# Output norm of a hybrid mLSTM and attention layer: variance from a ScalarE square, sums from the residual additions, and a same-engine lag in the kernel's own planner

## Chip, cores and metric

The kernel runs on one core of one Trainium2 chip. The metric is the device time of one execution in microseconds; the median of 3 runs before the change is 1039.39 us (1038.61 to 1039.49). Engines are named as in the profile: PE is TensorE, DVE VectorE, ACT ScalarE, POOL GpSimd, SP SyncE, whose queue issues nearly all of the transfers.

## What is computed

One inference step of one decoder layer for a prompt of 1024 tokens and 8 decode samples, width 1024. The stream is normalised and projected (`w_in`); one half of the width goes through an mLSTM (4 heads, chunks of 128 tokens), the other through sparse attention with three branches (compressed, selected, window), merged by gates. Both halves, each times a SiLU gate, are joined to `mix` and go through the output projection. The end, which the change is mostly about, is

```python
def layer_norm(x, g=None, b=None):
    mu = xf.mean(-1, keepdims=True)
    var = jnp.square(xf - mu).mean(-1, keepdims=True)
    y = (xf - mu) * lax.rsqrt(var + LN_EPS)
    ...

def residual_out(x, mix, gate, w_out, b_out, ln_g, ln_b):
    y = mix @ w_out + b_out
    return layer_norm(DEEPNORM_ALPHA * x.astype(jnp.float32) + gate * y, ln_g, ln_b)
```

## The kernel before

The work is written as some hundred Python generators ("lanes"), each a piece of the layer: projections of a weight block, score and value pieces of the attention, chunks of the mLSTM, loads. A planner sets the order in which their instructions are written out, and so the order of every engine's queue. `Plan.note` (from line 247 on) keeps a planned clock for each engine. It advances an engine by the cost of the instruction, from the latest of the engine's own clock and the ends of the writers of its inputs, each with a lag (`LAG`, 0.08 to 0.2 us by the engine that wrote). `Lanes.run` takes, among the lanes in order of rank, the first that is ready at TensorE's planned clock, and runs it to its next `yield`; `yield [x]` means "go on when x is planned to be there". `sooner((V, ...), (G, ...))` gives an element-wise operation to VectorE or GpSimd, whichever is planned to be done with it first, so a different planned clock also moves work between the two. The helper at line 308 emits every instruction, so all rows of the profile carry that line, and instructions are told apart by their tiles.

TensorE's bulk is `mm<-hh,wh` and its two companions (`hl`, `wl`): fp32 products are made of three matmuls of high and low parts, so each weight block needs `wh` (a ScalarE copy) and `wl` (a subtraction on GpSimd or VectorE). In the first 900 us this projection is interleaved with attention (`sc`, `tp`, `oo`) and mLSTM chunks (`nd` is a chunk's output, normalised with an rsqrt in small steps, `rs_v`, `rs_y`, `rs_t`, on VectorE or GpSimd).

The merge of the samples' attention (`sample_merge`, from line 1439) has a matmul that spreads `vs`, a copy of the new key and value rows, over partitions. The copy is issued right before the matmul.

The output projection (`output`, from line 2336 on) runs at the end. The weights come in 8 slices of 128 rows: `wof` (load, then the product with the gate on VectorE or GpSimd), `woh` (ScalarE copy), `wol` (difference, VectorE or GpSimd). The prompt is 8 row tiles t of 128 tokens. For each tile and each half i of the contraction (i = 1 first) the `mix` tile is loaded, multiplied with the attention's or mLSTM's gate, and split into `mixh` (ScalarE) and `mixl` (VectorE or GpSimd). 24 matmuls of 512 columns make one half, 48 a tile. The order of tiles is i = 1 for tiles 0 to 2, i = 0 for them, then tiles 3 to 7 with both halves. `res_load` brings the residual `xr` and adds alpha and the bias (`xr<-xr,bo`). With i = 0 done, VectorE adds each 512-column piece of the PSUM sum to `xr`, and the lane `finish` does the norm: statistics of two pieces and an aggregate (`lnst`, `fmv`), an rsqrt in ten small operations (`rs_v` to `frs`), minus mean times rsqrt (`fnm`), ScalarE's Identity with scale and bias, the product with `lg` (VectorE or GpSimd), the addition of `lb` (GpSimd) and the store. Tile 7 takes its statistics piece by piece (`last_st`) and splits the last steps between engines. The samples (`smp`) go through the same `finish` with 8 rows.

Of the kernel before, what the change touches and what calls it, by code (L numbers as in the profile page):

```python
# [11 lines left out]
AF = mybir.ActivationFunctionType  # L12
ALU = mybir.AluOpType
# [130 lines left out]
class Plan:  # L144
# [2 lines left out]

    LAG = {"PE": 0.2, "ACT": 0.15, "DVE": 0.13, "POOL": 0.08, "DMA": 0.0}
    TO = {"PE": 0.07, "POOL": 0.03}
    TICK = 10.24 / 3  # L150

    def __init__(self):
# [94 lines left out]
    def note(self, kind, op, a, kw):  # L247
        aps = [x for x in a if isinstance(x, bass.AP)] + [x for k, x in kw.items() if isinstance(x, bass.AP)]
        out = kw.get("out", a[0] if a else None)
        outs = [out] + ([kw["accum_out"]] if "accum_out" in kw else [])  # L250
        if "in_offset" in kw and kw["in_offset"] is not None:
            aps.append(kw["in_offset"].ap)
        ins = list(aps)
        for o in outs:
            ins.pop(next(i for i, x in enumerate(ins) if x is o))
        eng = kind
        waits = [(self.clock[kind], kind, "")]
        for x in ins:
            for c in self.cells(x):
                for e in self.wrote.get(c, ()):  # L260
                    if not (kind == "PE" and e[1] == "PE"):
                        waits.append((self.after(e, kind), e[1], c))
        for x in aps:
            if x.space == PSUM or any(x is o for o in outs):
                for c in self.cells(x):
                    waits += [(self.after(e, kind), k, c) for k, es in self.used.get(c, {}).items() if k != kind
                              for e in es]
        load = kind == "DMA" or op == "indirect_dma_start"
        if load and len(self.begun[kind]) >= 8:
            waits.append((self.begun[kind][-8][0], "RING", ""))  # L270
        t = max(w[0] for w in waits)
        if load:
            size = out.free_size() * 4 * out.partition_size() / 360.0e3
            run = min(x.ap[-1][1] if x.ap[-1][0] == 1 else 1 for x in [out] + ins)
            if run < 128 and kind == "DMA":
                size *= 2
            self.clock[kind] = t + (1.04 if kind == "POOL" else 0.475)
            eng = "DMA"
            e = [0.0, eng]
            self.transfer(self.clock[kind] + 0.65, size, e)  # L280
            self.begun[kind].append(e)
        else:
            c = self.cost(kind, op, t, out, ins, len(outs) > 1)
            e = [t + c, kind]
            eng = kind
            self.clock[kind] = t + c
            self.step_end = max(self.step_end, self.after(e, "PE"))
        for x in outs:
            for c in self.cells(x):
                self.wrote[c] = (self.wrote.get(c, []) if eng == "DMA" else [])[-7:] + [e]  # L290
        for x in aps:
            for c in self.cells(x):
                u = self.used.setdefault(c, {})
                u[eng] = (u.get(eng, []) if eng == "DMA" else [])[-7:] + [e]
# [60 lines left out]
def build(ctx, tc, I, O, dbg=None):  # L355
# [38 lines left out]
    def bank(tag, hold=False):  # L394

        def first():
            return min(idle(b) for b in range(8))
        if first() > plan.clock["PE"]:
            yield first
        while first() >= BIG:  # L400
            yield first
        return take(tag, hold)
# [69 lines left out]
        return t  # L472


    def rsqrt_steps(dst, var, n, eps, rows=slice(0, 128), eng=None):

        E = eng or V
        v = W([128, 4], "rs_v", "rs_v", 4)[rows, :n]
        y = W([128, 4], "rs_y", "rs_y", 4, I32)[rows, :n]
        t = W([128, 4], "rs_t", "rs_t", 4)[rows, :n]  # L480
        E.tensor_scalar(v, var, eps, None, op0=ALU.add)
        yield
        E.tensor_scalar(y, v.bitcast(I32), -0.5, 1597463007.0, op0=ALU.mult, op1=ALU.add)
        E.tensor_scalar(v, v, -0.5, None, op0=ALU.mult)
        yf = y.bitcast(F32)
        for i in range(3):
            yield
            if E is V and n == 1:
                V.scalar_tensor_tensor(t, yf, v, yf, op0=ALU.mult, op1=ALU.mult)
            else:  # L490
                E.tensor_tensor(t, yf, yf, op=ALU.mult)
                yield
                E.tensor_tensor(t, t, v, op=ALU.mult)
            yield
            d = dst if i == 2 else yf
            if E is V:
                V.scalar_tensor_tensor(d, t, 1.5, yf, op0=ALU.add, op1=ALU.mult)
            else:
                E.tensor_scalar(t, t, 1.5, None, op0=ALU.add)
                E.tensor_tensor(d, t, yf, op=ALU.mult)  # L500
# [938 lines left out]
    def sample_merge():  # L1439
# [7 lines left out]
                             start=(w == 0), stop=(w == 1), skip_group_check=True)  # L1447
        sn = C([128, 2], "sn")
        V.tensor_scalar(sn, ps[:, 0:2], BN0, NS, op0=ALU.add, op1=ALU.mult)
        ps = yield from bank("sc")  # L1450
        vs = H([8, 2, 2, 64], "vs")
        V.tensor_copy(vs, skv[:, 1:3, :, 1, :])
        T.matmul(ps[:, 0:256], kc("rb8", 8), vs.rearrange("p a k d -> p (a k d)"), start=True, stop=True)
        T.matmul(ps[:, 256:280], kc("rb8", 8), GS[:, 8:32], start=True, stop=True)
        vn = H([128, 2, 2, 64], "vn")
# [774 lines left out]
    og = {}  # L2230
    woh, wol = [None] * 8, [None] * 8

    def finish(r, rows, dst, last=None):

        mv = W([128, 2], "fmv", "fmv", 3)[rows]
        rs = W([128, 1], "frs", "frs", 3)[rows]
        nm = W([128, 1], "fnm", "fnm", 3)[rows]
        yield [r]
        if last is None:
            ln_stats(r, mv, rows)  # L2240
        else:
            V.bn_aggr(mv, last.rearrange("p a b -> p (a b)"))
        yield
        rsqrt(rs, mv[:, 1:2], 1, 1e-5, rows)
        V.scalar_tensor_tensor(nm, mv[:, 0:1], -1.0, rs, op0=ALU.mult, op1=ALU.mult)
        yield
        n = 1024 if last is None else 320
        a, b = slice(0, n), slice(n, 1024)
        S.activation(r[:, a], r[:, a], AF.Identity, bias=nm, scale=rs)
        (sooner((V, 1.2), (G, 3.5)) if last is None else G).tensor_tensor(r[:, a], r[:, a], og["lg"][rows, a], op=ALU.mult)  # L2250
        G.tensor_tensor(r[:, a], r[:, a], og["lb"][rows, a], op=ALU.add)
        if last is not None:
            V.scalar_tensor_tensor(r[:, b], r[:, b], mv[:, 0:1], og["lg"][rows, b], op0=ALU.subtract, op1=ALU.mult)
            V.scalar_tensor_tensor(r[:, b], r[:, b], rs, og["lb"][rows, b], op0=ALU.mult, op1=ALU.add)
            yield [r[:, b]]
            dma(dst[:, b], r[:, b])
        yield [r[:, a]]
        dma(dst[:, a], r[:, a])
# [77 lines left out]
    def output():  # L2336
# [65 lines left out]
        for t, i in [(t, i) for i in (1, 0) for t in range(3)] + [(t, i) for t in range(3, 8) for i in (1, 0)]:  # L2402
            if i == 0:
                yield from done("floads")
                load(t + 3)
            yield from done("w%d" % (2 + 5 * i), "mix%s%d" % ("ab"[i], t))
            hi, lo = mix.pop((t, i))
            for x, (m, tag) in enumerate(PIECES[t == 7]):
                m, n = slice(*m), m[1] - m[0]
                if i:  # L2410
                    po[t, x] = (yield from bank(tag or (["sc", "mm"][t % 2] if t != 2 else ["sc", "oo"][x]), True))[:, 0:n]
                ps = po[t, x]
                for k in range(4):
                    w = 4 * i + k
                    T.matmul(ps, hi[:, k], woh[w][:, m], start=(w == 4), stop=False)
                    T.matmul(ps, hi[:, k], wol[w][:, m], start=False, stop=False)
                    T.matmul(ps, lo[:, k], woh[w][:, m], start=False, stop=(w == 3))
                    if k % 2:
                        yield 0
                if i == 0:  # L2420
                    yield from done("res%d" % t)
                    xr = mix[t]
                    V.tensor_tensor(xr[:, m], ps, xr[:, m], op=ALU.add)
                    free(ps)
                    if t == 7:
                        ln_part(xr, last_st, m)
                    yield 0
            if i == 0:
                flags.add("out%d" % t)
                lanes.add(1, finish(xr, slice(0, 128), O["y_prompt"][0, 128 * t:128 * t + 128],  # L2430
                                     last_st if t == 7 else None))

    lanes.add(0, begin())
    lanes.run()
# [36 lines left out]
```

## Time and profile before

| | |
|---|---|
| median of 3 runs | 1039.39 us |
| profiled execution | 1039.46 us, span 1037.6 us |
| granted clock, mean | 0.967 of full |
| TensorE busy | 959.7 us (92%) |
| VectorE busy | 717.2 us (69%) |
| ScalarE busy | 530.2 us (51%) |
| GpSimd busy | 286.5 us (28%) |

Busy time is the union of an engine's instructions. The averages hide that the stages differ: from 1013 us on TensorE has nothing to do, and VectorE, at 69% overall, is busy in nearly all of the last 100 us. "Idle before, releaser" on a row is the time that the engine stood still ahead of that instruction, and the tile that it waited for. A number with x on a row of small instructions counts equal neighbours.

### The profile page before, as it was taken

What the parts mean: (1) busy time and instruction counts of PE and PEld (TensorE: products, weight loads), DVE (VectorE), ACT (ScalarE), POOL (GpSimd) and SP (SyncE); (2) the same over time, 40 slices, a digit from 0 to 9 for tenths busy, and PEclk for the clock granted to TensorE, in tenths of its full rate; (3) what the DMA queues carried; (4) which work ended last, traced back from release to release, by engine and by line L of the source; (5) the groups of instructions that cost most, each with busy time, mean ns of one, the idle gap of its engine ahead of it and who ended that gap; (6) DMA issues with size and microseconds to landing.
All of it is one profiled execution on the core that took longest, in us unless ns stands there. A gap on an engine that the chain in (4) does not pass through costs nothing.

```text
span 1037.6 us, 20058 instructions
## 1 busy us (share of the span) xinstructions
PE 959.7 (92%) x7338; PEld 864.9 (83%) x7338; DVE 717.2 (69%) x2266; ACT 530.2 (51%) x1329; POOL 286.5 (28%) x362
## 2 busy tenths in 40 slices
PE   4997899999999989999999999999999899989990
PEld 3786897989888889899999998899998889967780
DVE  4859864072323477789777788878784738999996
ACT  3557752143344656676667786666773321231111
POOL 6216423111453000110131001131012524253563
PEclk9988899999999989999999999999999989989996
DMA  8943419413698715311105111012102326479502
GB/s 329 408 189 117 148 70 361 151 50 118 221 326 286 216 55 165 111 57 37 47 11 157 29 47 38 25 36 74 47 33 85 113 65 191 142 264 362 168 22 81
DMA packets 85334, 141.42 MB, mean 136 GB/s; under 512 B 11657, under 2 KB 58286, under 8 KB 85108
## 3 DMA queue, kind: packets, MB, share of 16 engines
q1 hardware_dynamic: 76020, 106.59, 31.2%
q0 software_dynamic: 9216, 33.56, 9.0%
q8 instruction: 58, 0.95, 0.4%
q14 instruction: 40, 0.33, 0.1%
HBM read 117.73 MB, written 28.15 MB: 141 GB/s over the span
## 4 chain that ended last, share of the span: by engine, by line
PE 57%; DVE 11%; DMA 4%; issue 2%; POOL 2%; ACT 1%; POOLq 0%; SPq 0%; DVEq 0%; ACTq 0%
PE mm L308 27%; PE sc L308 13%; PE tp L308 9%; PE oo L308 7%; DVE xr L308 2%; DMA wof<-in_w_out 1%; DMA pgs<-in_cache_slc_kv,idx 1%; DVE smp L308 1%; DVE lnst L308 1%; DVE rs_t L308 1%; POOL wol L308 1%; DMA mg<-mgd 1%; DVE mixl L308 1%; DMA pgs<-in_cache_win_kv 1%; DVE rs_y L308 0%
## 5 line engine op out<-in xcount | busy, mean ns | idle before, releaser
L308 PE MATMUL mm<-hh,wh 128*128 128x344 f32 (+1 forms) x840 | 286.3, 341 | 0.0
L308 PE MATMUL mm<-hl,wh 128*128 128x344 f32 (+1 forms) x840 | 270.4, 322 | 0.0
L308 PE MATMUL mm<-hh,wl 128*128 128x344 f32 x816 | 262.6, 322 | 0.0
L308 POOL TENSOR_TENSOR wl<-wf,wh 128x1024 fp32r<-128x1024 f32 (+1 forms) x35 | 82.5, 2356 | 505.0 <-ACT wh L308 389.6
L308 PEld LDWEIGHTS mm<-hh,wh 128*128 128x128 f32 (+1 forms) x840 | 158.8, 189 | 12.1 <-issue 10.5
L308 PEld LDWEIGHTS mm<-hl,wh 128*128 128x128 f32 (+1 forms) x840 | 158.9, 189 | 0.7
L308 PEld LDWEIGHTS mm<-hh,wl 128*128 128x128 f32 x816 | 155.1, 190 | 0.0
L308 PE MATMUL oo<-pt,VT 128*64 128x128 f32 x1056 | 70.1, 276 | 0.0
L308 PE MATMUL sc<-kst,qs 128*128 128x448 f32 (+6 forms) x208 | 69.5, 343 | 0.3 <-DVE pt L308 0.3
L308 PE MATMUL sc<-kst,ql 128*128 128x448 f32 (+6 forms) x208 | 65.5, 325 | 0.0
L308 PEld LDWEIGHTS oo<-pt,VT 128*64 128x64 f32 x1056 | 58.1, 137 | 6.4 <-issue 5.2
L308 DVE COPY pt<-tp 128x512 f32<-128x512 f32 (+1 forms) x87 | 54.8, 645 | 9.9 <-PE tp L308 9.7
L308 ACT ACTIVATE pw<-pw,nbs 128x64 f32<-128x64 f32 (+2 forms) x112 | 54.6, 489 | 12.6 <-DVE tot L308 6.4
L308 ACT ACTIVATE pt<-tp 128x512 f32<-128x512 f32 (+1 forms) x73 | 39.8, 558 | 40.6 <-PE tp L308 40.4
L308 ACT ACTIVATE pa<-pa,nbs 128x384 f32<-128x384 f32 (+1 forms) x88 | 50.9, 580 | 14.6 <-DVE pa L308 12.4
L308 ACT ACTIVATE xh<-tp 128x512 fp32r<-128x512 f32 x64 | 38.0, 595 | 35.2 <-PE tp L308 34.9
L308 DVE TENSOR_TENSOR xl<-tp,xh 128x512 fp32r<-128x512 f32 x64 | 42.8, 679 | 14.3 <-ACT xh L308 14.0
L308 PE MATMUL tp<-KA,pgx 128*128 128x128 f32 x256 | 43.3, 293 | 2.8 <-ACT pgx L308 1.9
L308 ACT ACTIVATE ti<-sc,PKT 128x129 f32<-128x129 f32 x28 | 10.3, 369 | 67.3 <-DVE cx L308 67.3
L308 ACT ACTIVATE pp<-pp,nbs 128x64 f32<-128x64 f32 (+3 forms) x72 | 32.2, 449 | 22.7 <-DVE nbs L308 21.3
L308 PE MATMUL sc<-xl,w1h 128*128 128x256 f32 x128 | 38.3, 299 | 5.0 <-DVE xl L308 5.0
L308 PEld LDWEIGHTS sc<-kst,qs 128*128 128x128 f32 x208 | 39.8, 191 | 3.3 <-DVE pt L308 1.0
(506 smaller groups left out, 2285.0 us busy)
## 6 DMA issues: line engine op xcount, KB each, us to landing
wf<-in_w_blk SPq DMA_DIRECT2D x34, 512.0 KB
wada<-in_w_ada SPq DMA_DIRECT2D x24, 512.0 KB
wof<-in_w_out SPq DMA_DIRECT2D x16, 512.0 KB
xt<-in_x_prompt SPq DMA_DIRECT2D x8, 512.0 KB
pgs<-in_cache_win_kv SPq DMA_DIRECT2D x8, 512.0 KB
qf<-qtd SPq DMA_DIRECT2D x32, 128.0 KB
mix<-mxd SPq DMA_DIRECT2D x16, 256.0 KB
mix<-gtd SPq DMA_DIRECT2D x16, 256.0 KB
```

Of the source, the lines that this page charges most:

```text
L308: return f(*a, **kw)
```

## The change

Four things, of which the last reaches furthest:

1. For prompt tiles 0 to 6 the residual addition becomes a `tensor_tensor_reduce`, which adds the PSUM piece to `xr` and also sums the result into `osum` (two instructions: the operation and the read of its accumulator). The mean comes from the two sums (one small VectorE operation, negated), the variance from a ScalarE Square with the negated mean as bias and a row sum into `fmv` (its other output, `sq`, is not used). `rsqrt_steps` gets a factor, 1/1024, for it. Statistics and aggregate are gone for these tiles; tile 7 and the samples keep them.
2. `finish` now waits, in the plan, for ScalarE's Identity before the `lg` product is placed.
3. In `sample_merge` the copy to `vs` is issued first, and its lane yields before it takes a PSUM bank and issues the matmul.
4. The planner counts a lag (`OWN`, 0.08 to 0.1 us) between dependent instructions of the same engine on ScalarE, VectorE and GpSimd. Before, such a dependence had the engine's `LAG` as any other; transfers and TensorE had and have their own rule.

```diff
@@ class Plan
     LAG = {"PE": 0.2, "ACT": 0.15, "DVE": 0.13, "POOL": 0.08, "DMA": 0.0}
     TO = {"PE": 0.07, "POOL": 0.03}
+
+    OWN = {"ACT": 0.1, "DVE": 0.09, "POOL": 0.08}
@@ Plan.note
                 for e in self.wrote.get(c, ()):
-                    if not (kind == "PE" and e[1] == "PE"):
+                    if e[1] != kind:
                         waits.append((self.after(e, kind), e[1], c))
+                    elif kind in self.OWN:
+                        waits.append((e[0] + self.OWN[kind], kind, c))
@@ rsqrt_steps
-        E.tensor_scalar(v, var, eps, None, op0=ALU.add)
+        if scale is None:
+            E.tensor_scalar(v, var, eps, None, op0=ALU.add)
+        else:
+            E.tensor_scalar(v, var, scale, eps, op0=ALU.mult, op1=ALU.add)
@@ sample_merge
-        ps = yield from bank("sc")
         vs = H([8, 2, 2, 64], "vs")
         V.tensor_copy(vs, skv[:, 1:3, :, 1, :])
+        yield [vs]
+        ps = yield from bank("sc")
         T.matmul(ps[:, 0:256], kc("rb8", 8), vs.rearrange("p a k d -> p (a k d)"), start=True, stop=True)
@@ finish
-    def finish(r, rows, dst, last=None):
+    def finish(r, rows, dst, last=None, sums=None):
...
+        if sums is not None:
+
+            V.tensor_scalar(mv[:, 0:1], sums[:, 0:1], sums[:, 1:2], -1.0 / 1024, op0=ALU.add, op1=ALU.mult)
+            yield [mv]
+            sq = R([128, 1024], "sq")
+            S.activation(sq, r, AF.Square, bias=mv[:, 0:1], accum_out=mv[:, 1:2])
+            yield [mv]
+            rsqrt(rs, mv[:, 1:2], 1, 1e-5, rows, scale=1.0 / 1024)
+            V.scalar_tensor_tensor(nm, mv[:, 0:1], 1.0, rs, op0=ALU.mult, op1=ALU.mult)
...
         S.activation(r[:, a], r[:, a], AF.Identity, bias=nm, scale=rs)
+        if last is None:
+            yield [r[:, a]]
@@ output
-                    V.tensor_tensor(xr[:, m], ps, xr[:, m], op=ALU.add)
+                    if x == 0:
+                        sums = W([128, 2], "osum", "osum", 3)
+                    if t == 7:
+                        V.tensor_tensor(xr[:, m], ps, xr[:, m], op=ALU.add)
+                        ln_part(xr, last_st, m)
+                    else:
+                        V.tensor_tensor_reduce(out=xr[:, m], in0=ps, in1=xr[:, m], scale=1.0, scalar=0.0, op0=ALU.add,
+                                               op1=ALU.add, accum_out=sums[:, x:x + 1])
                     free(ps)
-                    if t == 7:
-                        ln_part(xr, last_st, m)
```

The instructions' order changes on every engine, mostly from about 360 us on. Three places follow. The line number before an operation is the helper's, 308 before and 312 after.

TensorE around the matmul of `vs` (`knew` scores the samples' new keys, `kst` the prompt's window; KS and GS are constants and gates). Before:

```order
L308 MATMUL mm<-hh,wl 128x344
L308 MATMUL sc<-knew,qbd 32x1 x16
L308 MATMUL sc<-vs,KS 128x256
L308 MATMUL sc<-GS,KS 128x24
L308 MATMUL sc<-kst,qs 128x320
L308 MATMUL sc<-kst,ql 128x320
```

and after the change, where the row of `knew` stands 25 rows above that of `vs`:

```order
L312 MATMUL mm<-hh,wl 128x344
L312 MATMUL sc<-kst,qs 128x256
L312 MATMUL sc<-kst,ql 128x256
L312 MATMUL sc<-kst,qs 128x320
L312 MATMUL sc<-kst,ql 128x320
L312 MATMUL sc<-vs,KS 128x256
L312 MATMUL sc<-GS,KS 128x24
```

24 rows of other work, projection and window scores, now stand between them.

VectorE in the mLSTM chunk near 820 us (`mva` is the chunk's variance on its way through GpSimd's rsqrt, `vx` the next chunk's values). Before:

```order
L308 TENSOR_TENSOR mva<-mva,den 128x4
L308 COPY vx<-tp 128x4x128
L308 TENSOR_TENSOR wof<-wof,gate 128x1024
L308 TENSOR_TENSOR wol<-wof,woh 128x1024 x2
L308 TENSOR_TENSOR mva<-mva,den 128x4
L308 TENSOR_SCALAR nd<-nd,mmv,mva 128x128 x4
```

and now:

```order
L312 TENSOR_TENSOR mva<-mva,den 128x4
L312 COPY vx<-tp 128x4x128
L312 TENSOR_TENSOR mva<-mva,den 128x4
L312 TENSOR_SCALAR nd<-nd,mmv,mva 128x128 x4
L312 TENSOR_SCALAR qm<-tp,g_106 128x512
```

The weight product `wof` and one `wol` have moved ahead, one `wol` to GpSimd.

VectorE at the additions of tile 5 in the output projection. Before:

```order
L308 TENSOR_TENSOR xr<-mm,xr 128x512
L308 TENSOR_TENSOR smp<-smp,lg 8x1024
L308 TENSOR_TENSOR xr<-xr,lg 128x1024
L308 BN_STATS lnst<-xr 128x6 x2
L308 BN_AGGR fmv<-lnst 128x2
```

and now:

```order
L312 ISA xr,osum<-mm,xr 128x512
L312 ISA osum 128x1
L312 TENSOR_TENSOR xr<-xr,lg 128x1024
L312 ISA xr,osum<-mm,xr 128x512
L312 ISA osum 128x1
L312 TENSOR_TENSOR mixl<-mix,mixh 128x512 x2
L312 TENSOR_SCALAR fmv<-osum 128x1
L312 TENSOR_SCALAR rs_v<-fmv 128x1
```

The two `mixl` are those of tile 7; before they were GpSimd's. The mean and the first step of the rsqrt, which needs ScalarE's sum of squares, follow each other without a row between them.

## Rows read from the trace of the kernel before

**Rows 1.** Busy time by stage, core 0; the columns are named in the first line.
```profile
core 0: us, PE busy (x) PEld busy (x) DVE busy (x) ACT busy (x) POOL busy (x), PEclk, DMA share, GB/s
400.00:600.00 200.00, 199.09 (x1682) 185.45 (x1682) 152.49 (x624) 142.23 (x417) 29.70 (x66) 1.00 0.24 72
...
900.00:940.00 40.00, 34.96 (x164) 29.46 (x163) 37.81 (x68) 11.60 (x16) 17.77 (x9) 0.91 0.83 274
940.00:1000.00 60.00, 60.00 (x275) 45.82 (x274) 56.78 (x101) 10.41 (x14) 30.50 (x14) 1.00 0.58 194
1000.00:1020.00 20.00, 13.58 (x83) 11.89 (x81) 18.02 (x47) 3.73 (x3) 9.71 (x5) 0.94 0.16 63
```

**Rows 2.** TensorE's waits: what for, us in total, times, longest.
```profile
PE tp L308 <- DVE nd L308: 5.9, 2, 4.2
...
PE sc L308 <- DVE vs L308: 3.0, 1, 3.0
PE sc L308 <- POOL wol L308: 2.9, 1, 2.9
```

**Rows 3.** Timeline of VectorE around 365 us, and busy time and clock behind it.
```profile
361.03 0.23 DVE L308 CUSTOM_DVE_ANT_0 pp<-sc,CBT 128x64 f32<-128x64 f32 x1 [3.22 <-POOL wl L308]
...
365.30 0.27 DVE L308 COPY vs<-skv 8x256 f32<-8x256 f32 x1
...
365.60:372.20 6.60, 6.57 (x23) 6.33 (x24) 4.09 (x24) 2.85 (x10) 0.00 (x0) 0.50 0.00 1
```

**Rows 4.** Timelines of VectorE and GpSimd around 820 us, and the stretch behind them.
```profile
820.92 2.44 DVE L308 TENSOR_TENSOR wol<-wof,woh 128x1024 fp32r<-128x1024 f32 x2
826.33 1.20 DVE L308 TENSOR_TENSOR mva<-mva,den 128x4 f32<-128x4 f32 x1 [2.98 <-POOL mva L308]
...
821.06 1.14 POOL L308 TENSOR_TENSOR rs_t<-rs_y 128x4 f32<-128x4 f32 x1
...
824.09 0.20 POOL L308 TENSOR_TENSOR rs_t<-rs_y 128x4 f32<-128x4 f32 x1
...
829.20:840.50 11.30, 11.30 (x63) 11.28 (x62) 2.69 (x6) 0.57 (x1) 2.37 (x1) 0.83 0.28 95
```

**Rows 5.** Timeline of GpSimd around 917 us, and the stretch behind TensorE's wait.
```profile
916.67 3.34 POOL L308 TENSOR_TENSOR wol<-wof,woh 128x1024 fp32r<-128x1024 f32 x1 [4.54 <-ACT woh L308]
...
920.07:925.70 5.63, 5.63 (x14) 4.50 (x15) 5.50 (x13) 1.06 (x1) 3.56 (x2) 0.54 0.87 261
```

**Rows 6.** Timelines of the output projection: VectorE, then GpSimd.
```profile
942.68 0.69 DVE L308 TENSOR_TENSOR xr<-sc,xr 128x512 f32<-128x512 f32 x1 [1.09 <-PE sc L308]
...
949.00 1.28 DVE L308 BATCH_NORM_STATS2 lnst<-xr 128x6 f32<-128x512 f32 x2
...
950.43 4.55 DVE L308 TENSOR_TENSOR mixl<-mix,mixh 128x512 fp32r<-128x512 f32 x2
...
1005.04 0.68 DVE L308 TENSOR_TENSOR xr<-mm,xr 128x512 f32<-128x512 f32 x1
...
1022.93 0.68 DVE L308 TENSOR_TENSOR xr<-sc,xr 128x512 f32<-128x512 f32 x1
...
951.71 2.71 POOL L308 TENSOR_TENSOR xr<-xr,lb 128x1024 f32<-128x1024 f32 x1
...
999.06 2.55 POOL L308 TENSOR_TENSOR mixl<-mix,mixh 128x512 fp32r<-128x512 f32 x2
...
1030.08 1.39 POOL L308 TENSOR_TENSOR xr<-xr,lb 128x320 f32<-128x320 f32 x1
```

**Rows 7.** Groups of instructions by shape: count, busy us, mean ns, idle before and releaser.
```profile
L308 DVE CUSTOM_DVE_ANT_0 pw<-sc,NB 128x256 f32<-128x256 f32 x32 | 13.4, 420 | 0.0
...
L308 DVE DVE_READ_ACCUMULATOR2_ANT nbs<- 128x1 f32 x224 | 18.6, 83 | 0.0
...
L308 DVE TENSOR_TENSOR xr<-xr,lg 128x1024 f32<-128x1024 f32 x4 | 4.9, 1225 | 2.1 <-ACT xr L308 2.0
...
L308 ACT ACTIVATE xr<-xr,fnm,frs 128x1024 f32<-128x1024 f32 x7 | 8.7, 1243 | 54.0 <-DVE fnm L308 54.0
...
L308 ACT ACTIVATION_READ_ACCUMULATOR pw<-pw,nbs 128x1 f32 x112 | 21.2, 189 | 0.0
```

More of the change, by code (lines that the diff above doesn't have):

```diff
@@ L472, in gather, with rsqrt_steps @@
         return t
-    def rsqrt_steps(dst, var, n, eps, rows=slice(0, 128), eng=None):
+    def rsqrt_steps(dst, var, n, eps, rows=slice(0, 128), eng=None, scale=None):
         E = eng or V
@@ L2238, in finish @@
         yield [r]
-        if last is None:
-            ln_stats(r, mv, rows)
-        else:
[L2242 to L2245, printed above, removed]
+        if sums is not None:
[6 more added lines that the diff above has]
+            V.scalar_tensor_tensor(nm, mv[:, 0:1], 1.0, rs, op0=ALU.mult, op1=ALU.mult)
+        else:
+            if last is None:
+                ln_stats(r, mv, rows)
+            else:
+                V.bn_aggr(mv, last.rearrange("p a b -> p (a b)"))
+            yield
+            rsqrt(rs, mv[:, 1:2], 1, 1e-5, rows)
+            V.scalar_tensor_tensor(nm, mv[:, 0:1], -1.0, rs, op0=ALU.mult, op1=ALU.mult)
         yield
@@ L2249, in finish @@
         S.activation(r[:, a], r[:, a], AF.Identity, bias=nm, scale=rs)
+        if last is None:
+            yield [r[:, a]]
         (sooner((V, 1.2), (G, 3.5)) if last is None else G).tensor_tensor(r[:, a], r[:, a], og["lg"][rows, a], op=ALU.mult)
@@ L2422, in output @@
                     xr = mix[t]
-                    V.tensor_tensor(xr[:, m], ps, xr[:, m], op=ALU.add)
+                    if x == 0:
[3 more added lines that the diff above has]
+                        ln_part(xr, last_st, m)
+                    else:
+                        V.tensor_tensor_reduce(out=xr[:, m], in0=ps, in1=xr[:, m], scale=1.0, scalar=0.0, op0=ALU.add,
+                                               op1=ALU.add, accum_out=sums[:, x:x + 1])
                     free(ps)
-                    if t == 7:
-                        ln_part(xr, last_st, m)
                     yield 0
@@ L2430, in output @@
                 lanes.add(1, finish(xr, slice(0, 128), O["y_prompt"][0, 128 * t:128 * t + 128],
-                                     last_st if t == 7 else None))
+                                     *([last_st] if t == 7 else [None, sums])))
     lanes.add(0, begin())
```

## The prediction

> **What bounds the kernel now.** I read the busy time by stage first. From 400 to 600 us TensorE is busy 199.09 of 200 us at full clock, and from 600 to 800 it is nearly the same: there the matmuls alone set the time. From 900 on this changes. VectorE is busy 37.81 of 40 us, and from 940 to 1000 both engines are full, 60.00 and 56.78 of 60; after 1000 TensorE has only 13.58 us left, so its last matmul ends near 1013.6, while VectorE goes on [rows 1]. So there are two bounds: TensorE's stream of matmuls with the few gaps in it, and in the last 95 us VectorE.
>
> For the first bound I read TensorE's waits: 5.9 us for nd (two waits, the longer 4.2), 3.0 for vs, 2.9 for wol [rows 2]. Each is followed by matmuls at a low clock, so a wait costs more than its length. The three places:
>
> At 365, VectorE had stood 3.22 us behind GpSimd's wl and came to the copy into vs only at 365.30; TensorE, with the vs matmul at the head of its queue, waited. From 365.60 to 372.20 the granted clock is then 0.50, that is 1.2 GHz [rows 3].
>
> At 820, the rsqrt of an mLSTM chunk runs as 15 small GpSimd steps beside VectorE's gate product and two wol. Steps that take 0.20 alone took 1.14 there, VectorE then waited 2.98 us for the result, and TensorE 4.2 for nd; the next 11.3 us ran at 0.83 [rows 2, 4].
>
> At 917, TensorE waits for a wol that GpSimd finished late (3.34 us), and 5.63 us at 0.54 follow [rows 2, 5].
>
> For the second bound I read VectorE's timeline from 942.68, the last place before the end where it waits for TensorE (1.09 us), to 1022.93, the first addition of row tile 7. It is 80.25 us with about 2 us idle [rows 6]. That addition's PSUM sums were ready near 1011 (a tile's 48 matmuls take 48 x 60.00 / 275 = 10.5 us [rows 1]; tile 7's end at 1013.6, this piece a quarter of them earlier), so it comes 12 us late. The end is the rest: tile 7's statistics and rsqrt, then the last GpSimd operation at 1030.08 [rows 6] and the store.
>
> **The change part by part.** The sum is made against the profiled execution, 1039.46 us, 0.07 above the median of three runs; its span is 1037.6, and the 1.86 outside I leave.
>
> *Norm on ScalarE.* Tiles 0 to 6 lose two statistics operations and an aggregate: 949.00 to 950.43, so 1.43 each [rows 6] and 7 x 1.43 = **10.0 us less** on VectorE. The reducing addition is not in this tail. Its nearest rows are the reducing operations with one PSUM input: 0.23 at 64 columns [rows 3] and 420 ns at 256 [rows 7], 1.0 ns per column, so 0.68 at 512, what the plain addition costs (0.69 [rows 6]). Its accumulator read is 83 ns [rows 7], 14 of them between 0 (hidden) and 1.2; I take **+1.2**, nothing in the row hiding it. The negated mean is one small operation, at most the 0.23 of rows 3; seven, between 0.7 and 1.6, I take **+1.2**.
>
> The square on ScalarE is not in the trace either. Nearest is the 1024-wide Identity, 1243 ns, plus an accumulator read of 189 [rows 7] and a hop each way: about 1.7 us in which VectorE waits if its next row is the rsqrt. By the order of the change that is so for tiles 0, 5 and 6, and about 0.4 of it for tile 4; for 1, 2 and 3 an addition, a split or a product stands between. That is 3 x 1.7 + 0.4 = **+5.5**, between 0 and 12. ScalarE is busy 10.41 of 60 us there [rows 1], so the square itself delays nobody else. The new wait before the lg product takes away the 2.0 us that VectorE stood for ScalarE at two of them [rows 7]: **-2.0**. Four lg products stay on VectorE (other tiles); two mix products fewer and two splits more cancel. Sum for the tail: -10.0 + 1.2 + 1.2 + 5.5 - 2.0 = **-4.1**.
>
> These prices hold only if nothing collides. Two splits at 950.43 took 4.55 us together, and end within 0.6 of GpSimd's lb, which began at 951.71 and ran 2.71 [rows 6]. The Trainium skill, GPSIMD Engine Reference, section "Key points", says that GpSimd shares its SBUF interfaces with VectorE and contends with VectorE instructions of two SBUF inputs. The trace agrees (4.55 for a pair); by that rule the reductions, with one PSUM input, lose nothing, but the splits that come to VectorE pay for every GpSimd operation beside them, which speaks against the change and is the third case below.
>
> *vs first.* In the new order the vs matmul stands 24 rows later on TensorE, and the copy is issued where it was. 24 matmuls at the mean of 199.09 / 1682 = 0.12 us [rows 1] are 2.8 us, so the wait of 3.0 all but goes, and with it most of the slow stretch, at most half of 6.6 = 3.3; I take 2. Together **-5**, between 0 (another wait takes its place) and -6.3.
>
> *Same-engine lag in the plan.* This writes the whole order anew, with the same work. At 820 the product and both wol leave VectorE's place between vx and mva; three of GpSimd's 15 steps had been stretched, by 0.94 each [rows 4], so its chain can end 2.8 us earlier. Of 4.2 + 11.3 x 0.17 = 6.1 us I take **-3.5**, between 0 and -6.1. At 917 one gate product and one wol go from VectorE to GpSimd, and nd comes 36 matmuls earlier; lost there are 2.9 + 5.63 x 0.46 = 5.5 us. But on SyncE's queue the load of weight slice 7, the one waited for, now stands behind the store that waits for VectorE's qm, so the wait shrinks and doesn't go, and VectorE is the bound next: **-2**, between -5.5 and +2, since four weight loads more fall into a stretch where the DMA engines are busy 0.83 already [rows 1]. VectorE waits for TensorE at 942.68, so what is won before that comes through.
>
> *New gaps.* From 360 on every engine's order differs, and in the TensorE-bound 400 us nothing hides a gap. The order does not show waits. The nearest rows are the old gaps: 3 to 4 us of wait and 2 of low clock each [rows 2, 3]. The bounds are 0 and four such (20); I take two shorter ones at 4 us, **+8**, against the three of this size that the old order has.
>
> Sum: -4.1 - 5 - 3.5 - 2 + 8 = **-6.6**, so 1032.9 us, rounded to **1033**.
>
> **Rivals.** Changes within 0.2% (2.1 us) are about what a measurement of this kernel can't tell from none.
>
> First, *the new order opens more gaps than it closes.* For it: four of five terms rest on gaps picked because they are there; the new ones can't be seen, and TensorE at 199 of 200 us has no slack. Against it: the planner made the old order too, and that has three. With four gaps (20 in place of 8) the sum is +5.4: **1045**; with three, 1040. Slower from 3.4 gaps on.
>
> Second, *VectorE catches up fully.* If contention in the tail falls with the load (the pair of splits at 950.43 alone lost 3.2 of its 4.55 us against two plain 512-wide operations at 0.68), tile 7's addition comes as its sums are ready, 12 us earlier: -12 for -4.1, and new gaps cost less: **1025**. Against it: GpSimd's share does not shrink.
>
> Third, the other side: *tile 7's two splits hold TensorE.* They ran on GpSimd at 999.06 (2.55 us) [rows 6]; in the new order they stand on VectorE behind tile 5's second addition, which ran at 1005.04. TensorE wants them near 1003 (10.5 before its end). VectorE's account up to that addition: five statistics gone (-7.2), reads and means +1.7, stalls +2.1, but four lg products earlier (4 x 1.22 [rows 7] = +4.9) and two mix products fewer (-1.3): about zero. So the splits end at 1007 alone, at 1010 or later beside GpSimd's lb. At 1007 TensorE's last sums are ready at 1017.5, before VectorE wants them near 1019; at 1010 they come at 1020.5, and a clock of 0.54 after the wait adds 2.6. The tail gain of 4.1 then becomes a loss of 1 to 3, and with one gap more than I take the result is **1042**. It decides from a split end of 1009 on.
>
> Fourth, *the lag changes little and the gains cancel:* -5 and -4 given back as gaps, **1039**.
>
> **How the numbers follow.** The forecast case, 1028 to 1037, has 0.56. More gaps 0.15, full catch-up 0.12, the held TensorE 0.09, no change 0.08. Faster by over 0.2% (below 1037.3): 0.56 less 0.02 at its edge, plus 0.12 and 0.02 of mild third cases, 0.68. Slower (above 1041.5): 0.12 of the first and 0.06 of the third, 0.18. The rest, 0.14, is the same. The range leaves out one in ten at either end: it reaches down to the catch-up case, 1025, and up to the mild ends of the first and third, 1042.
>
> **What would show it.** Right: no TensorE wait for vs, full clock from 366; the nd wait near 820 under 2 us; in the tail no statistics before tile 7, each reducing addition near 0.68 with a read near 0.08, a square near 1.25, VectorE idle for it at tiles 0, 5 and 6, and tile 7's first addition 4 us or more nearer to the last matmul. Wrong: new TensorE waits over 3 us between 400 and 900 with a clock below 0.9; VectorE still 12 us late at tile 7; or a TensorE wait for mixl near 1003.

## The result, and the profile after

The change is slower: 1047.63 us (median of 6 runs, 1045.77 to 1050.71) against 1039.44, a ratio of 1.0082 (95% interval 1.0064 to 1.0101), where 1033 was forecast. The profiled execution has a span of 1047.7 us.

Three points cut the span so that both orders have done the same work at each: TensorE's scores of the samples' new keys (`knew`, just ahead of the vs matmul), the first matmul of the output projection, and the last matmul. The timelines of TensorE, first of the kernel before:

```profile
362.19 0.43 PE L308 MATMUL sc<-knew,qbd 128*32 128x1 f32 x32
...
913.91 0.48 PE L308 MATMUL sc<-woh,mixh 128*128 128x512 f32 x1
...
1013.31 0.28 PE L308 MATMUL sc<-woh,mixl 128*128 128x256 f32 x1
```

and of the change:

```profile
366.18 0.43 PE L312 MATMUL sc<-knew,qbd 128*32 128x1 f32 x32
...
370.77 0.69 PE L312 MATMUL sc<-vs,KS 8*128 8x256 f32 x2
...
923.29 0.39 PE L312 MATMUL sc<-woh,mixh 128*128 128x512 f32 x1
...
932.00 0.80 PE L312 MATMUL sc<-wol,mixh 128*128 128x512 f32 x1 [6.03 <-DVE wol L312]
...
1016.01 0.50 PE L312 MATMUL sc<-woh,mixh 128*128 128x512 f32 x1 [1.69 <-ACT mixh L312]
...
1019.77 0.79 PE L312 MATMUL sc<-woh,mixl 128*128 128x512 f32 x1 [3.04 <-DVE mixl L312]
...
1033.34 0.28 PE L312 MATMUL sc<-woh,mixl 128*128 128x256 f32 x1
```

| us | before | change | difference |
|---|---|---|---|
| start to knew | 362.2 | 366.2 | +4.0, but it varies in runs of one order (below) |
| **middle**: knew to the first output matmul | 551.7 | 557.1 | +5.4 |
| **output on TensorE**: to the last matmul | 99.4 | 110.0 | +10.6 |
| **rest**: last matmul to the span's end | 24.3 | 14.4 | -9.9 |

The last two belong together, as the output stages: TensorE takes 10.6 us longer to its end, and VectorE, whose first addition of tile 7 came 9.6 us after the last matmul in the kernel before, has caught up. Their sum is 124.4 us against 123.7, so the norm's gain is used up there and not more. The net loss stands in the middle, and it is idle time of TensorE. TensorE's busy time from knew to the first output matmul, with the columns of [rows 1], before and then after:

```profile
362.19:913.91 551.72, 536.09 (x4294) 498.38 (x4294) 420.63 (x1628) 330.42 (x963) 106.82 (x199) 0.98 0.25 76
...
366.18:923.29 557.11, 535.08 (x4294) 494.00 (x4293) 426.58 (x1627) 331.39 (x965) 110.56 (x201) 0.99 0.25 75
```

The same matmuls take 536.1 and 535.1 us; TensorE is idle 15.6 us of this stretch before and 22.0 after.

Within the middle, the busy time of the change answers to [rows 1]:

```profile
400.00:600.00 200.00, 195.91 (x1653) 180.41 (x1651) 157.55 (x641) 143.94 (x425) 25.58 (x65) 1.00 0.23 69
600.00:800.00 200.00, 194.27 (x1644) 176.64 (x1643) 152.67 (x617) 131.04 (x401) 29.57 (x68) 1.00 0.16 46
```

TensorE is idle 4.1 and 5.7 us there, where it was idle 0.9 and 1.8. Its waits from 362 to 924 us, to be held against [rows 2]:

```profile
PE sc L312 <- DVE wt L312: 2.8, 1, 2.8
PE tp L312 <- DVE d L312: 2.6, 1, 2.6
PE tp L312 <- DVE pa L312: 2.6, 3, 1.2
PE tp L312 <- DVE mva L312: 2.0, 1, 2.0
PE tp L312 <- DVE pp L312: 1.8, 2, 1.3
PE tp L312 <- ACT pw L312: 1.5, 3, 0.7
PE tp L312 <- DVE pw L312: 1.5, 2, 1.1
PE tp L312 <- ACT NPT L312: 1.3, 1, 1.3
PE oo L312 <- DVE pt L312: 1.2, 1, 1.2
PE mm L312 <- POOL sm L312: 1.0, 1, 1.0
PE tp L312 <- DVE nd L312: 1.0, 2, 0.6
...
```

The wait for vs is gone, and nd has fallen from 5.9 to 1.0. In all there are 24 waits where there were nine, none above 2.9 us and most near 1 or below: 21.9 us in place of 15.5, of which 5.7 at tiles that TensorE had waited for by 0.5 us or more before too (d, pp, nd, ti), so 16.2 us, in eighteen waits, are new. Two of them were followed back to VectorE. Timelines of the change, VectorE and GpSimd, ahead of the waits for pa (TensorE at 609.80) and wt (816.15):

```profile
607.05 3.35 DVE L312 TENSOR_SCALAR pa<-pa,ef 128x384 f32<-128x384 f32 x3
...
606.94 2.40 POOL L312 TENSOR_TENSOR wl<-wf,wh 128x1024 fp32r<-128x1024 f32 x1 [25.41 <-ACT wh L312]
...
810.95 2.32 DVE L312 TENSOR_TENSOR den<-den,PKT 128x4 f32<-128x4 f32 x1
...
810.86 2.40 POOL L312 TENSOR_TENSOR wof<-wof,gate 128x1024 f32<-128x1024 f32 x1
```

An operation on 4 columns takes 2.32 us and ends as GpSimd's product ends. The planner has no term for this; it books such an operation at its own length. Not every wait is like this: VectorE has an operation held by 0.3 us or more beyond the shorter ones of its form, with GpSimd at work beside it, in the 6 us ahead of 16 of the 24 waits (14.4 of the 21.9 us), and none ahead of the other eight. Such meetings are not new either. The kernel before has the same one, at the same operation, without a TensorE wait for wt behind it:

```profile
814.76 2.32 DVE L308 TENSOR_TENSOR den<-den,PKT 128x4 f32<-128x4 f32 x1
...
814.63 2.42 POOL L308 TENSOR_TENSOR wl<-wf,wh 128x1024 fp32r<-128x1024 f32 x1
```

By the same count it has 25 of them in the middle, which lose 33 us in sum, against 27 and 41 us in the change. So the orders differ in where the meetings fall, and by 8 us in what they lose by them. That they make the new waits is an argument from their place in time; no experiment took them out of the middle.

The tail, VectorE at tiles 0 and 1:

```profile
955.40 0.21 DVE L312 TENSOR_SCALAR fmv<-osum 128x1 f32<-128x1 f32 x1
956.92 0.15 DVE L312 TENSOR_SCALAR rs_v<-fmv 128x1 f32<-128x1 f32 x1 [1.31 <-ACT sq L312]
...
965.45 0.68 DVE L312 CUSTOM_DVE_ANT_0 xr<-mm,xr 128x512 f32<-128x512 f32 x1
966.06 0.08 DVE L312 DVE_READ_ACCUMULATOR2_ANT osum<- 128x1 f32 x1
966.06 1.78 DVE L312 TENSOR_TENSOR mixl<-mix,mixh 128x512 fp32r<-128x512 f32 x2
...
1030.90 0.68 DVE L312 TENSOR_TENSOR xr<-sc,xr 128x512 f32<-128x512 f32 x1
```

The reducing addition costs 0.68, its read starts with the next operation and costs nothing, and VectorE waits 1.31 us for a square with nothing between (the same at tiles 5 and 6). Tile 7's first addition comes 2.4 us before the last matmul; in the kernel before it came 9.6 after it [rows 6].

### The profile page after: what moved, and what is told of

Read it like the earlier page. It is cut to its first block, busy times and chain, and to the rows that moved or that the text cites. A ratio compares the mean times of both kernels' runs of the same rounds, so it can differ in the third digit from the quotient of the medians.

```text
span 1047.7 us, 20095 instructions
## 1 busy us (share of the span) xinstructions
PE 964.1 (92%) x7338; PEld 865.4 (83%) x7338; DVE 712.0 (68%) x2265; ACT 537.3 (51%) x1343; POOL 288.7 (28%) x363
## 5 line engine op out<-in xcount | busy, mean ns | idle before, releaser
L312 DVE COPY pt<-tp 128x512 f32<-128x512 f32 (+1 forms) x83 | 52.7, 651 | 11.2 <-PE tp L312 11.2
L312 DVE TENSOR_TENSOR xl<-tp,xh 128x512 fp32r<-128x512 f32 x64 | 42.6, 678 | 16.0 <-ACT xh L312 15.7
L312 PE MATMUL sc<-xh,w1h 128*128 128x256 f32 x128 | 43.0, 336 | 0.0
```

Source lines behind the costliest of these rows:

```text
L312: return f(*a, **kw)
```

## The experiments

Each ratio is to runs of the kernel before, taken beside it on the same chip. Beside experiments 9 to 14 that kernel took 1054 to 1055 us; in the profiles of these experiments knew comes at 374.7 to 380.9 us, where it came at 359.2 to 366.2 in all others, so there only ratios and stages are compared. "Middle", "output on TensorE" and "rest" are the stages above, the last two together the output stages (124.4 in the change, 123.7 before). The intervals of 3, 4 and 10 overlap that of the change, and those of 1, 8, 9 and 14 overlap each other, so the order among these is not shown by the times alone.

**1. The norm alone.** The change without `OWN` and with the lane of vs as before:

```diff
-    OWN = {"ACT": 0.1, "DVE": 0.09, "POOL": 0.08}
...
-                    if e[1] != kind:
+                    if not (kind == "PE" and e[1] == "PE"):
                         waits.append((self.after(e, kind), e[1], c))
-                    elif kind in self.OWN:
-                        waits.append((e[0] + self.OWN[kind], kind, c))
...
+        ps = yield from bank("sc")
         vs = H([8, 2, 2, 64], "vs")
         V.tensor_copy(vs, skv[:, 1:3, :, 1, :])
-        yield [vs]
-        ps = yield from bank("sc")
```

> Only part 1 and 2 of the change (reducing additions, square on ScalarE, the wait before lg), with the planner and the vs lane of before: TensorE's and SyncE's orders are those of before, and VectorE's differ from the first residual addition on. Theory A (the loss comes from the new order ahead of the output projection, the norm by itself helps): 1035 to 1040, VectorE reaches tile 7's first addition 2 to 5 us earlier, unless tile 7's splits, which are on VectorE here too, hold TensorE. Theory B (the norm itself costs, through waits for the square and the splits that move to VectorE): 1043 to 1049.

Ratio 0.9978 (0.9963 to 0.9993). VectorE's stretch of 80.25 us, from tile 0's second addition to tile 7's first [rows 6], is 77.28 (940.80 to 1018.08): 3.0 less, where I had worked out 4.1. Output on TensorE and rest together are 122.0 us against 123.7. The norm helps, and theory B falls.

**2. The lag alone.** The kernel before with the hunks of `OWN` only.

```diff
+    OWN = {"ACT": 0.1, "DVE": 0.09, "POOL": 0.08}
...
-                    if not (kind == "PE" and e[1] == "PE"):
+                    if e[1] != kind:
                         waits.append((self.after(e, kind), e[1], c))
+                    elif kind in self.OWN:
+                        waits.append((e[0] + self.OWN[kind], kind, c))
```

> Only part 4 (the same-engine lag in the plan). The norm and the vs lane are those of before; the order differs from the start. Theory A: TensorE comes to the output projection 5 to 12 us later than before, and the time is 1043 to 1051. Theory B: the order matters little, 1037 to 1041.

Ratio 1.0127 (1.0092 to 1.0161). More than theory A had it, though TensorE comes to the output projection 5 us later, at the low end of its range, and most of the loss stands elsewhere than in the change: middle 553.5, output on TensorE 114.7, rest 18.0 (together 132.7 against 123.7). Its TensorE waits in the output projection:

```profile
PE sc L312 <- ACT mixh L312: 5.7, 1, 5.7
PE sc L312 <- ACT woh L312: 4.7, 1, 4.7
PE sc L312 <- DVE wol L312: 4.3, 1, 4.3
```

**3. Tile 7's splits on GpSimd.** In the change:

```diff
-            split(*mix[t, i], p, (V, 0.6), (G, 1.2))
+            split(*mix[t, i], p, *([(G, 1.2)] if t == 7 else [(V, 0.6), (G, 1.2)]))
```

> The change with tile 7's two splits forced to GpSimd, where they were before; every other row stays but one lg product, which goes to VectorE in exchange. Theory of the held TensorE: the wait for mixl of 3.0 us before tile 7 and most of the slow clock behind it go, TensorE ends 3 to 6 us earlier, and the time falls by 2 to 5. Rival (VectorE would be late for tile 7 anyway): within 1 us of the change.

Ratio 1.0063 (1.0042 to 1.0084), some 2 us less than the change, the least that the theory asked for; its mechanism failed, for the wait did not go:

```profile
PE sc L312 <- DVE wol L312: 5.4, 1, 5.4
PE sc L312 <- POOL mixl L312: 3.7, 1, 3.7
PE sc L312 <- ACT mixh L312: 2.3, 1, 2.3
```

So it isn't the engine alone that makes the splits late; their place in the order does it (experiments 9 and 10).

**4. Gate products of slices 1 and 2 on VectorE.** In the change:

```diff
-            sooner((V, 1.2), (G, 2.3)).tensor_tensor(w, w, og["gate"], op=ALU.mult)
+            (V if k in (1, 2) else sooner((V, 1.2), (G, 2.3))).tensor_tensor(w, w, og["gate"], op=ALU.mult)
```

It goes back to these rows of the change, VectorE and GpSimd ahead of the wait of 6.03 us:

```profile
925.38 2.66 DVE L312 SCALAR_TENSOR_TENSOR tz<-tz,zv 128x344 f32<-128x344 f32 x1
928.08 2.54 DVE L312 SCALAR_TENSOR_TENSOR to<-to,tz 128x344 f32<-128x344 f32 x1
...
930.73 1.22 DVE L312 TENSOR_TENSOR wol<-wof,woh 128x1024 fp32r<-128x1024 f32 x1
...
924.36 5.89 POOL L312 TENSOR_TENSOR wof<-wof,gate 128x1024 f32<-128x1024 f32 x2 [2.12 <-DMA wof<-in_w_out]
```

> The change with the gate products of weight slices 1 and 2 forced from GpSimd to VectorE (TensorE's, ScalarE's and SyncE's orders stay; some later splits and differences change between VectorE and GpSimd in the plan's own way). Theory: the 6.0 us wait for slice 7's wol comes from two small VectorE operations, tz and to, that were stretched from 1.3 to 5.2 us beside these two GpSimd products; so the wait shrinks to 1 to 3 us and TensorE is 3 to 5 us earlier at tile 0. Rival (the late load behind the store of qm sets it): the wait stays at 5 to 6 us.

Ratio 1.0059 (1.0036 to 1.0081). The waits for slice 7 fall from 6.0 to 0.9 (woh) and 2.2 (wol), with the load still where the change has it (issued behind the store of qm, 5.2 us ahead of the first output matmul, in both): the place of the gate products made most of that wait, not the late load that I had named. How much of it is the collision stays open. The pair tz and to still takes 0.51 and 2.54 us in 4, `to` now held beside a wol, and the products themselves take 1.22 on VectorE where GpSimd had 5.89 for two. Output on TensorE and rest together are 123.9 us, 0.5 less, so little of it reaches the end.

**5. vs alone.** The kernel before with the two moved lines and the new `yield [vs]`:

```diff
-        ps = yield from bank("sc")
         vs = H([8, 2, 2, 64], "vs")
         V.tensor_copy(vs, skv[:, 1:3, :, 1, :])
+        yield [vs]
+        ps = yield from bank("sc")
```

> Only part 3 (vs first). The planner's costs and the norm are those of before, but from the vs lane on (360 us) the order differs on every engine. Theory of the place (the 3.0 us wait and the slow clock behind it are given back): 1033 to 1036. Theory of the re-plan (what an edit of the order costs or gives at other places outweighs the place that it mends): anywhere from 1036 to 1050, with the loss in the output projection.

Ratio 0.9999 (0.9980 to 1.0018). The wait for vs is gone and nothing is won: the middle is 553.0, 1.3 us longer than before, so the new order gives the place's gain back there and a little more; the output stages are 120.2, 3.5 less, and knew comes 2.0 later. The time is that of the re-plan, but its loss isn't in the output projection, where that theory put it.

**6, 7 and 12. A nudge that means nothing.** The kernel before with VectorE's lag changed in the third digit:

```diff
-    LAG = {"PE": 0.2, "ACT": 0.15, "DVE": 0.13, "POOL": 0.08, "DMA": 0.0}
+    LAG = {"PE": 0.2, "ACT": 0.15, "DVE": 0.132, "POOL": 0.08, "DMA": 0.0}
```

(0.126 in the second, 0.128 in the third).

> The kernel before with one number of the planner changed by 1.5%: VectorE's lag 0.132 us in place of 0.13. Nothing is computed in another way and no cost of the plan is meant to be better or worse; some 500 of TensorE's 4273 rows stand elsewhere. Theory of chance (the order before is a lucky one of many, any new one is slower): 1042 to 1052. Theory of the same-engine lag (this rule makes worse plans, a mere nudge does not): 1036 to 1041.

> The same nudge the other way and larger: VectorE's lag 0.126 us; some 700 rows of TensorE stand elsewhere. Theory of chance: 1042 to 1052. Theory of the same-engine lag: 1036 to 1041.

> A third nudge of the planner before: VectorE's lag 0.128 us in place of 0.13, some 570 rows of TensorE elsewhere. The first two nudges gave 0.2% and 1.2% more time. Theory of chance: 1039 to 1052, with new TensorE waits in the output projection. Theory that a nudge is as good as none: 1036 to 1039.

1.0021 (1.0006 to 1.0036), 1.0124 (1.0090 to 1.0158) and 1.0035 (1.0015 to 1.0055). All three are slower, and the second as much as the lag alone. The first even has a shorter middle (546.4), and loses it in the output stages (129.6). The second's middle is 552.6 and its output stages 132.8, with these TensorE waits from 918 us on:

```profile
PE sc L308 <- DVE mixl L308: 8.5, 2, 5.4
PE sc L308 <- DVE wol L308: 4.6, 1, 4.6
PE sc L308 <- ACT woh L308: 1.5, 1, 1.5
```

The third has no stage that is longer by over 0.5 us behind 375 us in its profile (552.2, then 122.6 together); the profile is of its fastest execution, 5.7 us under its median, and where its 0.35% lies is open. Three draws are few, but they are enough to say that a loss of 1.2% needs no fault in the rule.

**8. The norm alone, tile 7's splits on GpSimd** (the edits of 1 and 3).

> The norm alone, as in the first experiment, with tile 7's two splits forced to GpSimd, where they are in the kernel before. The norm alone still had a TensorE wait of 1.7 us for a split of tile 7 on VectorE, and VectorE came to tile 7's first addition 5 us after the last matmul. Theory of the held TensorE: the wait goes and VectorE has 1.3 to 3 us less to do, so 1033 to 1035. Rival (GpSimd is then late with lb, and the end is the same): 1036 to 1038.

Ratio 0.9968 (0.9952 to 0.9985). The time came as expected, by another way: VectorE's stretch is 74.5 us (941.66 to 1016.15) in place of 80.25, while the wait for mixl grew to 5.9 us, output on TensorE to 105.2, and the rest fell to 13.6. VectorE's own work is what counted.

**9 and 10. Tile 7's splits one tile earlier**, in the norm alone (9) and in the change (10):

```diff
-                yield from done("out%d" % (t - 2))
+                yield from done("out%d" % (t - 3 if t == 7 else t - 2))
```

> The norm alone, with tile 7's splits one tile earlier in the plan (after tile 4's additions instead of tile 5's); TensorE's and SyncE's orders stay those of the kernel before. In the norm alone TensorE waited 1.7 us for a split of tile 7, and 5.9 us where the splits were forced to GpSimd. Theory of the held TensorE: no wait for mixl at tile 7, the last matmul as early as before (99.4 us after the first one of the output projection), and 1030 to 1034. Rival (the end is set by VectorE's rsqrts and GpSimd's lb whatever TensorE does): 1034 to 1037.

> The change with tile 7's splits one tile earlier in the plan; TensorE's and SyncE's orders stay those of the change. Theory: its waits for mixh and mixl of tile 7 (1.7 and 3.0 us) and the slow clock behind them go, the output projection on TensorE is 6 to 9 us shorter, and the time falls by 4 to 8 us to 1040 to 1044. Rival: within 2 us of the change.

0.9970 (0.9953 to 0.9988) and 1.0045 (1.0020 to 1.0071). The norm alone gains under 1 us: TensorE ends as early as the theory had it, and the time is the rival's (0.9970 of 1039.4 is 1036). The change gains some 3.8 us by its ratio, just short of what was expected. In both the waits for tile 7 are gone; in the change only slice 7 is left:

```profile
PE sc L312 <- DVE wol L312: 5.8, 1, 5.8
```

Output on TensorE is 99.4 in 9, as before, and 101.7 in 10, 8.3 us shorter than in the change. The rest grows to 21.7 and 20.2, because VectorE is the bound again. So the held TensorE, which looked like 5 us of waits and a clock of 0.66 from 1016 to 1026, was worth about 2.5 us at the end (124.4 to 121.9), and in the norm alone nearly nothing: 8 and 9 are equal.

**11. Both repairs in the change** (10 and 4).

> The change with both repairs: tile 7's splits one tile earlier, and the gate products of weight slices 1 and 2 on VectorE. Theory (the two places hold nearly all of what the change loses in the output projection, and the norm gains there): 1036 to 1041, no slower than the kernel before by over 0.2%. Rival (the gaps ahead of the output projection are what counts): 1042 to 1046.

1.0035 (1.0012 to 1.0058). A miss for the theory: the output stages are 121.3 us, 2.4 better than before, and the kernel is still slower. What is left is ahead of the output projection: 2.9 us in the middle by the one profile, the rest of the 3.6 not located.

**13 and 14. The lag in one stage only.** A switch in the planner, turned where the output projection's loop begins; 13 is the change with it on up to there, 14 the change with vs as before and the switch on from there:

```diff
+    own = True
...
-                    if e[1] != kind:
+                    if e[1] != kind or not (self.own or kind == "PE"):
...
         yield from done("proj", "w7")
+        plan.own = False
```

(True and False exchanged in 14).

> The change, with the same-engine lag counted only up to the start of the output projection: TensorE's order ahead of it is that of the change, and from there on the planner counts as before. Theory of the middle (the change loses its time between 362 us and the output projection, in small waits for attention tiles, and about nothing behind it): 557 us from the first matmul of knew to the first of the output projection (551.7 before), and 0.4 to 0.9% slower than before. Rival (the order of the output projection loses it): no slower than before by over 0.3%.

> The norm of the change, the order of the kernel before up to the output projection (TensorE's and SyncE's orders are those of before throughout), and the same-engine lag counted only from there on. Theory of the middle: 546 to 552 us from knew to the output projection and 119 to 123 us behind it, so 0.1 to 0.4% faster than before, like the norm alone. Rival: slower than before by 0.3% or more.

1.0102 (1.0066 to 1.0139) and 0.9968 (0.9940 to 0.9996); middle 557.1 and 551.0. The loss goes with the order ahead of the output projection. With the order of before up to there, the change's norm and lag together are faster than before, as fast as 8 and 9. TensorE's busy time in the middle repeats the two kernels' (13 like the change, 14 like the kernel before):

```profile
375.10:932.16 557.06, 535.21 (x4294) 494.01 (x4293) 426.60 (x1627) 331.26 (x965) 110.69 (x201) 0.99 0.25 76
...
380.92:931.91 550.99, 535.35 (x4295) 497.61 (x4294) 421.09 (x1628) 330.51 (x963) 106.93 (x199) 0.98 0.25 76
```

13 is slower than its theory had it (0.4 to 0.9%), which had "about nothing" behind the middle: its output stages are 127.0 us, 3.3 more than before, 14's are 119.8. With 1 and the change these make four versions with the same norm:

| ratio to before (output stages, us) | lag not counted in the output projection | lag counted there |
|---|---|---|
| order of before up to there | 0.9978 (122.0), experiment 1 | 0.9968 (119.8), experiment 14 |
| order of the change up to there | 1.0102 (127.0), experiment 13 | 1.0082 (124.4), the change |

The order ahead costs 1.1 to 1.2% in either column, 12 to 13 us, and the rule of the lag within the output projection nothing that is clear of noise. Of these some 6 us are in the middle and 4.6 to 5.0 in the output stages, where the order ahead uses up what the norm gives.

Over all profiles TensorE's idle time in the middle is steady by order: 22.0, 21.5, 21.1, 21.5, 20.5 and 21.9 us in the six with the change's order (its own, 3, 4, 10, 11 and 13), 15.6, 14.7, 15.7, 15.2 and 15.6 in the five with that of before (its own, 1, 8, 9 and 14). Means 21.4 and 15.4: **6.0 us** of the measured 8.2. The middle itself has 557.1, 558.9, 557.2, 557.4, 554.6 and 557.1 against 551.7, 545.7, 551.7, 551.5 and 551.0 us; the 545.7 of experiment 1 is not a better order but quicker matmuls (531.0 us busy in place of 536.1, at a granted clock of 0.99 in place of 0.98). The start shows no difference that its own spread would not cover. Neither edit makes the middle's loss by itself: the idle time there is 16.5 us with the lag alone (2) and 17.4 with vs alone (5).

## Why the prediction was wrong

The sum went wrong in two places of nearly equal size. In the middle its terms (-5, -3.5, +8) make -0.5, and the profiles show +5.4. In the output stages (-4.1, -2) they make -6.1, and the profiles show +0.7.

- **New gaps** (+8) is the first step that failed: the waits that a new order opens were put at half of what they are. I took two gaps after the pattern of the old ones. The change has 16.2 us of new waits in the middle, eighteen small ones in place of a few large, against 9.8 us closed (nd 4.9, vs 3.0, the others under 1 each). This is my first rival, put at 0.15, though that had gaps of 3 to 4 us. With 16 for 8, and +0.7 for -6.1, the sum would be +8.2; that this meets the measured 8.2 is luck, for the middle by it would be +7.5.
- **Slice 7** (-2) is the second: it had the wrong sign and the wrong reason. The wait grew from 2.9 to 6.0, through the two gate products on GpSimd ahead of it (experiment 4), not through the load. With tile 7's splits it used up the norm's gain.
- **The third rival** (tile 7's splits hold TensorE) came as described, with waits of 1.7 and 3.0 us, at 1016 and 1020 and not near 1003, but cost about 2.5 us, since VectorE sets the end.
- **The norm on ScalarE** (-4.1) was about right: 3.0 us in experiment 1, and 5.8 with tile 7's splits on GpSimd in 8. The terms inside were off in size: reads 0 instead of +1.2, the wait for a bare square 1.31 instead of 1.7, and the two extra splits, which I had set against two products, cost 2.8 by these two experiments. VectorE's splits took 2.1 us each in experiment 1, as in the kernel before (2.0).
- **vs first** (-5) was right at its place (no wait, clock 1.00 from 362 to 400, 0.91 before) and worth nothing in sum (experiment 5), because the edit re-plans all that follows.
- **The lag at 820** (-3.5): nd waits fell by 4.9 us, the one at 820 from 4.2 to 0.6. Right at its place.

Nearly every sign that I had named for being right came: no wait for vs, nd under 2, additions of 0.68, VectorE idle for the square at tiles 0, 5 and 6, tile 7's addition 12 us nearer to the last matmul. Of the signs of being wrong only the wait for mixl came; no new wait between 400 and 900 was over 3 us. The signs tested the places that I had named, and not the sum.

The general error was to price a re-plan by the places one can see. A place with a gap is known to be bad, so a new order looks better there; the places where it is worse were not to be seen in the rows that I had. Three nudges without meaning say what the estimate should have started from: 0.2 to 1.2% slower.

## What to carry to other kernels

Treat the order of a kernel that a planner draws, and that was kept because it measured well, as one good draw; an edit ahead of its bound draws another. None of the six new orders here (experiments 2, 5, 6, 7 and 12, and the change) was faster than the old one. Judge an edit on the old order first: here the norm, with TensorE's order left as it was, gives 0.2 to 0.3%, and the same norm in the change's order loses 0.8%. And where two engines slow each other, a planner that books each operation at its own length leaves it to chance where the gaps fall.

## What the runs showed of the hardware that I had not expected

- With TensorE's order unchanged, its idle time in the middle repeats closely (14.7 to 15.7 us in five executions). The first 360 us don't repeat: knew came at 359.2, 363.2 and 366.2 in three executions of one order, and at 374.7 to 380.9 in experiments 9 to 14. The cause is open.
- VectorE waits behind GpSimd's operation even with one tensor input: three `pa` operations of 384 columns by a scalar took 3.35 us beside a `wl` of 2.40. The Trainium skill, GPSIMD Engine Reference, section "Key points", says that GpSimd contends with VectorE instructions in a two-port mode as well as with those of two SBUF inputs. The rows fit this, but no run here shows an instruction's mode.
- A read of VectorE's accumulator, 83 ns in the table of groups [rows 7], starts together with the next operation in the timeline (both at 966.06), so it cost no time there.
